# One weight sum of a seven-product matrix multiplication, computed on VectorE instead of GpSimd

## The chip, the cores and the metric

The kernel runs on one core of a Trainium2 chip. A core has five engines with a queue of instructions each: TensorE (PE) multiplies matrices into PSUM, VectorE (DVE), ScalarE (ACT) and GpSimd (POOL) work on tiles, and SyncE (SP) only issues transfers here. The metric is the device time of one execution in microseconds; lower is better.

## What is computed

One layer of a hybrid decoder, in float32, on 512 prompt rows and 32 sample rows. The change touches its last part, a gated MLP with a short causal convolution:

```python
h = _rmsnorm(x, g_pre_ffn) * (1 + sc_f) + sh_f
g, new_f = _causal_dwconv(h @ w_gate, st_f, conv_f_w)
f = silu(g) * (h @ w_up)
x = x + ga_f * _rmsnorm(f @ w_down, g_post_ffn)
```

The model width is 1024, the MLP's inner width 2816, that is 22 column blocks of 128. All 544 rows are processed together, in two halves of 272.

## The kernel before

Every float32 product is made of three matmuls: each operand is split into a high part (a copy rounded to the matmul's type, ScalarE, L242 for weights) and a low part (the difference, VectorE's or GpSimd's subtraction, L243), and `mm3` adds high x high, high x low and low x high (L246 to L248).

The first three column blocks of the gate and up matrices are multiplied plainly. From block 3 on each block j is a **pair**: the 2 x 2 arrangement of (gate or up) by (half of the rows) is computed by seven block products instead of eight, as in Strassen's scheme in Winograd's form. It needs four sums of weight blocks and four sums of activations. The weight sums S1 to S4 of a pair lie in one tile of 2048 columns, `gs`; the plain weights in another, `ga`. S1 and S3 are made by DMAs that add to what lies in `gs` (`s_dma`, issued by GpSimd, L1215 and L1216). S2 = S1 - W (a sign is folded into the stored weights) is an addition on VectorE (L1221), S4 is made from S2 by a further addition on GpSimd (L1222).

The weights of a pair are seven units of 512 columns (four 128x128 blocks), split by `w_prep(i, j)`: i = 0 takes units 0 and 1 from `ga`, i = 1 units 2 and 3 (the two DMA sums) from `gs`, i = 2 units 4 and 5 (S2 and S4) from `gs`, i = 3 unit 6 from `ga`. Each product is twelve matmuls of 128x272 on one unit (`p_step`), and the order on TensorE is products 1, 5, 7, 2, 6, 3, 4, on units 0, 3, 2, 1, 4, 5, 6. Product 1 of pair j + 1 follows product 4 of pair j.

The other engines work between these products in an order that is written out by hand; each engine takes its instructions in that order. For pair j of the loop it is, with the line that the profile shows:

- VectorE: the difference c21 of the pair before (L1280); the low half of units 4 and 5 (L243, called lo2 below); S2 of pair j + 1 (L1221); two taps of the convolution of the pair before (L1295) and two small ones (L1302); the low half of unit 6 (L243, zl); diff_75 (L1269); the gating product (L1314) and, for a pair of index below 6, the low half of a split of f (L1311); the low half of units 2 and 3 of pair j + 1 (lo1); c11 (L1272); the low half of units 0 and 1 of pair j + 1 (lo0); c12 (L1276, L1277).
- ScalarE: the high half before each low half (L242; for f L1310), copies of products out of PSUM (L1265), the first tap (L1290), a small tap (L1300), the silu of the pair before (L1305), a small state copy (L1286) that stands between c12 and the high half of units 4 and 5.
- GpSimd: S4 of pair j + 1 (L1222); a small copy (L1268); the two accumulating DMAs for pair j + 2 (L1215, L1216); c22 (L1283), which waits for ScalarE's copy of product 6; a small copy (L1287).

Pair 3 runs inside an order of its own, interleaved with the end of the plain blocks; there the steps `S` and `L0` make the sums of pairs 3 and 4. In the loop, pair j makes the sums of pair j + 1, from pair 4 to pair 20. So S2 and S4 are made 19 times, for pairs 3 to 21. Four tiles of the ring hold `ga` and `gs` of two pairs, and the plain loads of a further pair go into a tile when its last reader is done. After pair 21 the down projection follows on TensorE.

Of the kernel before, what the change touches and what calls it, by code (L numbers as in the profile page):

```python
# [104 lines left out]
def body(tc, nc, A):  # L105
# [3 lines left out]
    pe, act, dve, pool, sp = nc.tensor, nc.scalar, nc.vector, nc.gpsimd, nc.sync  # L109
# [1105 lines left out]
        pool.dma_start(t[:, :512], w[:, :512], accum_op=OP.add)  # L1215
        pool.dma_start(t[:, 512:1024], w[:, 1536:], accum_op=OP.add)  # L1216

    def s_add(j, eng=pool):

        w, t = ring.get(("ga", j)), ring.get(("gs", j))  # L1220
        dve.tensor_add(t[:, 1024:1536], t[:, 512:1024], w[:, :512])  # L1221
        eng.tensor_add(t[:, 1536:], t[:, 1024:1536], w[:, 512:1024])  # L1222
# [108 lines left out]
    def first_pair(k, i):  # L1331

        j = NA
        if k == "K":
            step(lambda: p_step(j, i))
        elif k == "X":
            a, r = {1: ("a", "p1"), 5: ("b", "p5"), 6: ("a", "u2")}[i]
            step(lambda: copy_out(j, a, r))
            if i == 6:
                step(lambda: acb.give(("a", j)))  # L1340
        elif k == "V":
            for fn in {7: (diff_75,), 1: (c11,), 2: (c22,), 3: (c12, states)}[i]:
                step(lambda fn=fn: fn(j))
        elif k == "R":
            n = j if i == 3 else j + 1
            step(lambda: w_prep(i, n), ("ga" if i in (0, 3) else "gs", n))
        elif i == 0:
            step(lambda: s_add(j + 1), ("ga", j + 1), ("gs", j + 1))
        else:
            step(lambda: s_dma(j + 2), ("gs", j + 2))  # L1350

    for w in FLOW.split():
        k, i = w[0], [int(c) for c in w[1:] if c.isdigit()]
        eng = pool if w[-1] == "p" else dve
# [14 lines left out]
        elif k == "u":  # L1369
            step(lambda i=i: up_ev(*i))  # L1370
        elif w == "To":
            step(t_open)
        elif k in "AB":
            step(lambda i=i, k=k, eng=eng: (t_add if k == "A" else t_split)(i[0], eng))
        elif k == "S":
            step(lambda: s_add(NA), ("ga", NA), ("gs", NA))
        elif k == "D":
            step(lambda i=i: s_dma(i[0]), ("gs", i[0]))
        elif k == "G":
            step(lambda i=i, eng=eng: w_prep(i[0], NA, eng), ("ga" if i[0] in (0, 3) else "gs", NA))  # L1380
        elif k == "s":
            step(lambda i=i: silu(*i))
        elif k == "d":
            s_adc(i[0])
        elif k == "f":
            step(ada_fin)
        elif k == "C":
            step(close_xy)
        elif k in "KXVRL":
            first_pair(k, i[0])  # L1390
        elif k == "N":
            step(lambda i=i: fill(int("".join(map(str, i)))))
        elif k == "P":
            step(lambda i=i[0]: (bk.append(Q["sc"][i]), acb.free.append(len(bk) - 1)))
        else:
            assert w == "o", w
            step(open_p3)
            step(lambda: ring.add_tiles([Q["x"][0].rearrange("p c t -> p (c t)")], ("adc",)))
# [20 lines left out]
    def s_sums(j):  # L1419
        step(lambda: s_add(j), ("ga", j), ("gs", j))  # L1420
# [53 lines left out]
    j = NFF - 1  # L1474
# [208 lines left out]
```

## Time and profile before

| | |
|---|---|
| median of three runs | 730.06 us (729.93 to 732.63) |
| the profiled execution's own time | 731.16 us |
| its span | 729.4 us |
| busy in the span: TensorE, VectorE, ScalarE, GpSimd | 95%, 66%, 48%, 36% |
| mean granted clock of TensorE | 0.985 of full speed |

The time of an execution holds the span, from the first to the last instruction of the profile, and something around it. "PE" is a matmul, "PEld" a weight load. Times of single instructions count from the span's start. A matmul's duration includes its way through the array, so that successive matmuls overlap; other instructions overlap their successor by up to 0.1 us in the same way.

### The profile page before, as it was taken

Reading aid. Unit: us, or ns where it says so; the run is one execution under the profiler, and the core shown is the slowest. Engines: PE = TensorE matmul, PEld = TensorE weight load, DVE = VectorE, ACT = ScalarE, POOL = GpSimd, SP = SyncE. Lnnn points to the kernel's source line nnn. Section 1 sums busy time; section 2 is a strip of 40 time slices with the busy share of each in tenths; the row PEclk is TensorE's granted clock in tenths of the full one; section 3 lists DMA queues with packets and bytes.
Section 4 is the critical chain, followed back from the end, with each engine's and each line's share of the span. In section 5 each row is a group of like instructions: output and inputs, shape, how many; then the busy total and the mean of one; then the engine's idle time right before and its main releaser. Section 6 shows DMA issues by size and latency. Waiting matters only on the chain.

```text
span 729.4 us, 15203 instructions
## 1 busy us (share of the span) xinstructions
PE 693.3 (95%) x6108; PEld 648.9 (89%) x6108; DVE 482.0 (66%) x902; ACT 351.2 (48%) x721; POOL 262.1 (36%) x294
## 2 busy tenths in 40 slices
PE   8997999899999989997997999999999999999994
PEld 8895778877879779987997999999999999999993
DVE  4859799787345463467878888888888882222353
ACT  4432454535453436572665566655665662322430
POOL 3753234222332353465434425444544100100224
PEclk9999999999999999999999999999999999999997
DMA  9979964668657546174436576677666626130012
GB/s 352 420 257 266 392 229 136 255 234 318 268 225 260 204 174 236 60 262 168 113 73 155 150 190 162 171 187 181 159 179 149 239 105 239 58 116 1 1 38 87
DMA packets 44231, 136.17 MB, mean 187 GB/s; under 512 B 12688, under 2 KB 15008, under 8 KB 37504
## 3 DMA queue, kind: packets, MB, share of 16 engines
q1 hardware_dynamic: 36160, 117.47, 45.3%
q0 software_dynamic: 7280, 17.03, 11.3%
q8 instruction: 48, 0.79, 0.4%
q10 hardware_dynamic: 720, 0.69, 0.3%
q14 instruction: 23, 0.19, 0.1%
HBM read 127.99 MB, written 7.18 MB: 185 GB/s over the span
## 4 chain that ended last, share of the span: by engine, by line
PE 75%; DVE 11%; POOL 4%; issue 3%; ACT 3%; DMA 2%; SPq 0%; POOLq 0%; ACTq 0%; DVEq 0%
PE bk L246 18%; PE bk L248 18%; PE bk L247 18%; PE bk L736 2%; PE sc L248 2%; PE sc L247 2%; PE sc L246 2%; DVE cv L755 2%; PE sc L696 2%; PE bk L668 1%; DVE stl L243 1%; DMA ring<-in_w_in 1%; PE bk L653 1%; ACT sth L242 1%; POOL rr L274 1%
## 5 line engine op out<-in xcount | busy, mean ns | idle before, releaser
L243 DVE TENSOR_TENSOR stl<-ring,sth 128x1024 fp32r<-128x1024 f32 (+2 forms) x96 | 111.7, 1170 | 84.4 <-ACT sth L242 82.9
L242 ACT ACTIVATE sth<-ring 128x1024 fp32r<-128x1024 f32 (+3 forms) x122 | 118.6, 997 | 58.4 <-PE bk L247 51.5
L247 PE MATMUL bk<-xl,sth 128*128 128x272 f32 x424 | 123.7, 292 | 0.0
L246 PE MATMUL bk<-xh,sth 128*128 128x272 f32 x360 | 108.6, 302 | 4.5 <-DVE bigq L565 3.8
L248 PE MATMUL bk<-zh,stl 128*128 128x272 f32 x360 | 104.6, 291 | 4.3 <-DVE stl L243 4.3
L246 PE MATMUL bk<-zh,sth 128*128 128x272 f32 x360 | 104.5, 290 | 1.2 <-ACT sth L242 1.2
L248 PE MATMUL bk<-xh,stl 128*128 128x272 f32 x360 | 105.6, 293 | 0.0
L247 PE MATMUL bk<-zl,sth 128*128 128x272 f32 x360 | 104.0, 289 | 0.1
L243 POOL TENSOR_TENSOR stl<-ring,sth 128x1024 fp32r<-128x1024 f32 (+1 forms) x26 | 60.8, 2339 | 91.0 <-ACT sth L242 83.2
L247 PEld LDWEIGHTS bk<-xl,sth 128*128 128x128 f32 x424 | 81.7, 193 | 0.1
L246 PE MATMUL bk<-th,sth 128*128 128x272 f32 x280 | 80.9, 289 | 0.0
L248 PE MATMUL bk<-th,stl 128*128 128x272 f32 x280 | 80.7, 288 | 0.0
L247 PE MATMUL bk<-xh,sth 128*128 128x272 f32 x280 | 80.3, 287 | 0.0
L246 PEld LDWEIGHTS bk<-xh,sth 128*128 128x128 f32 x360 | 69.5, 193 | 9.2 <-issue 4.1
L248 PEld LDWEIGHTS bk<-zh,stl 128*128 128x128 f32 x360 | 68.0, 189 | 5.2 <-DVE stl L243 5.2
L246 PEld LDWEIGHTS bk<-zh,sth 128*128 128x128 f32 x360 | 68.0, 189 | 2.1 <-ACT sth L242 1.7
L248 PEld LDWEIGHTS bk<-xh,stl 128*128 128x128 f32 x360 | 69.6, 193 | 0.0
L247 PEld LDWEIGHTS bk<-zl,sth 128*128 128x128 f32 x360 | 68.1, 189 | 0.3 <-POOL zl L1060 0.3
L247 PEld LDWEIGHTS bk<-xh,sth 128*128 128x128 f32 x280 | 52.8, 188 | 0.0
L248 PEld LDWEIGHTS bk<-th,stl 128*128 128x128 f32 x280 | 52.6, 188 | 0.0
L246 PEld LDWEIGHTS bk<-th,sth 128*128 128x128 f32 x280 | 52.6, 188 | 0.0
L755 DVE SCALAR_TENSOR_TENSOR cv<-apad,vec,cv 128x512 f32<-128x512 f32 x60 | 50.3, 838 | 1.7
(335 smaller groups left out, 1708.8 us busy)
## 6 DMA issues: line engine op xcount, KB each, us to landing
ring<-in_ada SPq DMA_DIRECT2D x15, 1024.0 KB, 9.5
ring<-in_w_gu SPq DMA_DIRECT2D x57, 256.0 KB, 5.4
ring<-in_kc SPq DMA_DIRECT2D x16, 896.0 KB, 4.9
ring<-in_vc SPq DMA_DIRECT2D x16, 896.0 KB, 6.8
ring<-in_w_dn SPq DMA_DIRECT2D x11, 1024.0 KB, 4.9
ring<-in_w_in SPq DMA_DIRECT2D x10, 1024.0 KB, 11.1
ring<-in_w_gu SPq DMA_DIRECT2D x19, 512.0 KB, 5.5
ring<-in_w_gu POOLq DMA_DIRECT2D x38, 256.0 KB, 5.8
```

The costliest lines, as they stand in the source:

```text
L242: act.activation(hi, r[:, a:a + n, :], AF.Copy)
L243: eng.tensor_sub(lo, r[:, a:a + n, :], hi.bitcast(F32))
L246: pe.matmul(acc, wh, rh, start=start, stop=False, skip_group_check=more)
L247: pe.matmul(acc, wh, rl, start=False, stop=False, skip_group_check=more)
L248: pe.matmul(acc, wl, rh, start=False, stop=stop, skip_group_check=more)
L274: pool.tensor_tensor(r[:, :3 * nh], v[:, :3 * nh], mhalf[:, :3 * nh], op=OP.pow)
L653: pe.transpose(tp[:, b * 128:b * 128 + 128], e[:, b * 128:b * 128 + 128], idn)
L668: pe.matmul(pv[64 * s:64 * s + 64, :128], P[f"vt{hp % 2}"][:, b, 64 * s:64 * s + 64], pts[s][:, b, :], start=b == 0, stop=b == qb, tile_po ...
L696: pe.matmul(sc2[32 * b:32 * b + 32, bank, off:off + n], P["bigq"][:, hp, 4 * g + b, :], rhs, start=first[bank] == i, stop=last[bank] == i, ...
L736: pe.matmul(pv[32 * b:32 * b + 32, :256], lhs, rhs, start=kb == 0, stop=kb == KB, tile_position=(0, 32 * b))
L755: dve.scalar_tensor_tensor(cv[:, j, :NP], ap_[:, j, k:k + NP], V("caw", j * WA + k), cv[:, j, :NP], op0=OP.mult, op1=OP.add)
```

## The change

S4 of each pair by seven products is computed by VectorE, directly behind S2, instead of by GpSimd. It is one default argument; no caller passes another engine:

```diff
-    def s_add(j, eng=pool):
+    def s_add(j, eng=dve):
 
         w, t = ring.get(("ga", j)), ring.get(("gs", j))
         dve.tensor_add(t[:, 1024:1536], t[:, 512:1024], w[:, :512])
         eng.tensor_add(t[:, 1536:], t[:, 1024:1536], w[:, 512:1024])
```

The second addition reads what the first writes. All other instructions keep their engines and their order.

## Rows read from the trace of the kernel before

**Rows 1.** The page: the span, and the busy time, share of the span and number of instructions of each engine.

```profile
span 729.4 us, 15203 instructions
PE 693.3 (95%) x6108; PEld 648.9 (89%) x6108; DVE 482.0 (66%) x902; ACT 351.2 (48%) x721; POOL 262.1 (36%) x294
```

**Rows 2.** Busy time by stretch: an early pair (411.40 to 422.90 us) and a late one. The stretch, its length, then the busy time of PE, PEld, DVE, ACT and POOL with their instructions, the granted clock, the DMA engines' share and GB/s.

```profile
411.40:422.90 11.50, 10.67 (x85) 10.45 (x84) 9.72 (x17) 6.73 (x12) 3.94 (x7) 1.00 0.61 149
...
465.00:475.50 10.50, 10.50 (x86) 10.50 (x86) 8.85 (x16) 6.19 (x11) 4.85 (x7) 1.00 0.74 173
```

**Rows 3.** The chain that ended last, in order of time, two pieces that stand at the same place of the pair, six pairs apart: start, us, what.

```profile
507.36 0.13 PE bk L247
...
570.56 0.13 PE bk L247
```

**Rows 4.** The timeline of TensorE, its matmuls that came after an idle time: start, us, instruction, and in brackets the idle time before it and what ended it. The first is in pair 5, the second in pair 7.

```profile
401.19 0.40 PE L248 MATMUL bk<-zh,stl 128*128 128x272 f32 x1 [1.69 <-DVE stl L243]
...
424.48 0.40 PE L248 MATMUL bk<-zh,stl 128*128 128x272 f32 x1 [0.86 <-DVE stl L243]
```

**Rows 5.** The timeline of VectorE, c12 at the end of pair 5, pair 6's end (424.35), pair 7 from lo2 (425.94) to its c12 (434.47), and lo0 in pair 8 (443.02). A row with x2 holds two instructions from the first's start to the second's end.

```profile
412.70 0.40 DVE L1276 TENSOR_TENSOR bk<-bk,u 128x240 f32<-128x240 f32 x1
...
424.35 0.40 DVE L1276 TENSOR_TENSOR bk<-sc,u 128x240 f32<-128x240 f32 x1
...
425.94 1.23 DVE L243 TENSOR_TENSOR stl<-ring,sth 128x1024 fp32r<-128x1024 f32 x1 [0.76 <-ACT sth L242]
427.09 0.69 DVE L1221 TENSOR_TENSOR ring<-ring,ring 128x512 f32<-128x512 f32 x1
427.69 1.53 DVE L1295 SCALAR_TENSOR_TENSOR gy<-bk,vec,gy 128x511 f32<-128x511 f32 x2
...
429.60 0.68 DVE L243 TENSOR_TENSOR zl<-ring,zh 128x512 fp32r<-128x512 f32 x1
...
431.42 1.22 DVE L243 TENSOR_TENSOR stl<-ring,sth 128x1024 fp32r<-128x1024 f32 x1
...
432.91 1.64 DVE L243 TENSOR_TENSOR stl<-ring,sth 128x1024 fp32r<-128x1024 f32 x1
434.47 0.40 DVE L1276 TENSOR_TENSOR bk<-bk,u 128x240 f32<-128x240 f32 x1
...
443.02 1.22 DVE L243 TENSOR_TENSOR stl<-ring,sth 128x1024 fp32r<-128x1024 f32 x1
```

**Rows 6.** The timeline of VectorE in a late pair, the two instructions before which it was idle longest.

```profile
456.12 0.44 DVE L1280 TENSOR_TENSOR fraw<-sc,u 128x272 f32<-128x272 f32 x1 [0.95 <-PE sc L248]
...
458.63 1.53 DVE L1295 SCALAR_TENSOR_TENSOR gy<-bk,vec,gy 128x511 f32<-128x511 f32 x2 [0.33 <-ACT gy L1290]
```

**Rows 7.** The timeline of GpSimd in pairs 7 and 8: S4, the first DMA issue, c22 of pair 7 and c22 of pair 8.

```profile
427.91 1.30 POOL L1222 TENSOR_TENSOR ring<-ring,ring 128x512 f32<-128x512 f32 x1 [2.81 <-issue]
...
429.29 0.85 POOL L1215 DMA_DIRECT2D ring<-in_w_gu  x1
...
432.70 0.77 POOL L1283 TENSOR_TENSOR fraw<-p,u 128x272 f32<-128x272 f32 x1 [1.67 <-DVE stl L243]
...
443.05 1.83 POOL L1283 TENSOR_TENSOR fraw<-p,u 128x272 f32<-128x272 f32 x1 [1.89 <-ACT u L1265]
```

**Rows 8.** The timeline of ScalarE: the high halves of units 2, 3 and of units 0, 1 of pair 8 (two instructions), the copy of product 6 of pair 7, and the high half of units 4 and 5 in pair 8.

```profile
430.35 1.99 ACT L242 ACTIVATE sth<-ring 128x1024 fp32r<-128x1024 f32 x2
432.24 0.37 ACT L1265 ACTIVATE u<-bk 128x272 f32<-128x272 f32 x1
...
434.98 1.06 ACT L242 ACTIVATE sth<-ring 128x1024 fp32r<-128x1024 f32 x1
```

**Rows 9.** The instructions that write or read the tile gy: the taps' durations in ns, least, median and longest, and first and last start.

```profile
L1295 DVE SCALAR_TENSOR_TENSOR gy<-bk,vec,gy x38: 740/749/750, 392.8 to 587.2; 128x511 f32<-128x511 f32 x19, 128x510 f32<-128x510 f32 x19
```

**Rows 10.** The timelines of VectorE and GpSimd around the sums of pair 3: two subtractions before, two after, and S4.

```profile
366.11 1.35 DVE L1210 TENSOR_TENSOR xh<-y,th 128x544 fp32r<-128x544 f32 x2
...
369.12 2.45 DVE L1210 TENSOR_TENSOR xh<-y,th 128x544 fp32r<-128x544 f32 x2
...
368.14 2.21 POOL L1222 TENSOR_TENSOR ring<-ring,ring 128x512 f32<-128x512 f32 x1 [2.25 <-DVE ring L1221]
```

**Rows 11.** The same timelines in pairs 3 and 4: GpSimd's memset in front of a DMA issue, S2 of pair 4, lo2 in pair 4, S2 of pair 5.

```profile
375.61 0.10 POOL L1139 MEMSET fraw<- 128x2 f32 x1 [3.98 <-DVE xl L1171]
...
382.19 0.69 DVE L1221 TENSOR_TENSOR ring<-ring,ring 128x512 f32<-128x512 f32 x1 [2.06 <-DMA ring<-in_w_gu]
...
390.82 1.23 DVE L243 TENSOR_TENSOR stl<-ring,sth 128x1024 fp32r<-128x1024 f32 x1 [0.78 <-ACT sth L242]
392.17 0.69 DVE L1221 TENSOR_TENSOR ring<-ring,ring 128x512 f32<-128x512 f32 x1
```

**Rows 12.** Who waited for whom between 363 and 600 us, of TensorE and of VectorE: us in total, times, longest.

```profile
PE bk L248 <- DVE stl L243: 4.3, 4, 1.7
...
DVE fraw L1280 <- PE bk L248: 6.6, 7, 1.0
```

**Rows 13.** The timeline of VectorE, lo0 for pair 21 and the first waits in pair 21.

```profile
569.18 1.22 DVE L243 TENSOR_TENSOR stl<-ring,sth 128x1024 fp32r<-128x1024 f32 x1
...
571.99 0.44 DVE L1280 TENSOR_TENSOR fraw<-bk,u 128x272 f32<-128x272 f32 x1 [0.95 <-PE bk L248]
...
574.50 0.75 DVE L1295 SCALAR_TENSOR_TENSOR gy<-bk,vec,gy 128x511 f32<-128x511 f32 x1 [0.94 <-ACT gy L1290]
```

## The prediction, made before the changed kernel ran

> **What bounds the kernel now.** I read the page first, then the busy time by stretch, then who waits for whom, then single instructions of a few pairs. The page [rows 1] shows TensorE busy for 95% of the span and VectorE for 66%; by this average VectorE has room. But the change touches one stage only, the pairs by seven products (about 363 to 585 us), and there the picture changes along the way. The stretches [rows 2] show one early and one late pair: in the early one TensorE is not full (10.67 of 11.50 us), in the late one it is (10.50 of 10.50), and VectorE works 9.72 and 8.85 us.
>
> The chain of work that ended last gives the late pace: the same place in the pair at 507.36 and, six pairs on, at 570.56 [rows 3], so 10.53 us for a pair, all on TensorE. The early pace is VectorE's: TensorE stands still for 1.69 and, two pairs on, for 0.86 us [rows 4] at the same place, the first matmul of a pair that needs the low half of weight unit 0. I call that low half lo0; it is one VectorE subtraction of 128x1024 (L243), like lo2 (S2 and S4's own split) at the pair's begin and lo1. The later of these stalls ends at 424.48, in pair 7. It is the last of the four times that TensorE waits for L243 in this stage [rows 12].
>
> VectorE's own loop explains both. Its first instruction on product 3 (L1276) comes at 412.70, 424.35 and 434.47 [rows 5]: 11.65 us for pair 6, which still carries a split of f for a small index, and 10.12 us for pair 7, which doesn't. 11.65 is above TensorE's 10.53, 10.12 below it; so TensorE waits up to pair 7 and VectorE afterwards: in a late pair it waits 0.95 us for TensorE and 0.33 us for ScalarE [rows 6]. The whole question is whether pair 7 and its successors stay under 10.53 us.
>
> **The change part by part.** *S4 leaves GpSimd.* There it takes 1.30 us and has waited 2.81 us for S2 [rows 7]. Its reader is ScalarE's split of S2 and S4 in the next pair, at 434.98 [rows 8], 5.8 us after S4's end, so its length was never on the path. Behind it in GpSimd's queue stand a small copy (L1268) and the two accumulating DMA issues for the pair after next; these can come up to 3 us earlier. That costs nobody: the issues at 429.29 ran beside VectorE's zl (429.60, two SBUF operands), which took the 0.68 us that S2 of the same size takes with no issue beside it [rows 5, 7].
>
> *S4 arrives on VectorE.* The nearest row is S2 itself: same shape, same tiles, 0.69 us, and the next instruction starts 0.60 us after its start [rows 5]. But S4 reads what S2 writes. The two taps L1295 are such a dependent couple: together 1.53 us at 0.75 us each [rows 5, 9], so the second starts 0.78 after the first, 0.03 after its end. S2 then holds S4 for 0.69 + 0.03 = 0.72 us, S4 lasts 0.60 to the next start: 0.72 us more per pair. Bounds: 0.60 if the dependence is free, 0.84 if the taps too had to wait for S4's end. I take 0.72, the price of the one dependent couple that the loop shows.
>
> The Trainium skill, VectorE: DVE Perf Modes, section The DRAIN you can't avoid, has a measurement in which a semaphore between chained VectorE operations costs nothing extra. By that, S4 would add 0.60 us and the sum below would be 4.4 us; by the row it is 0.72 and 6.6, and I keep the row, since its couple has a true dependence.
>
> *What hides it?* In the early pairs nothing. S4 stands right behind S2, and everything VectorE does up to lo0 stands behind S4 in order: the taps, the silu that ScalarE makes of them, lo1, lo0. The one idle time of that loop, 0.76 us before lo2 [rows 5], lies in front of S2 and is ScalarE's answer to L1276, so it moves along.
>
> **The sum, in order.**
> *Pair 3.* Here S4 on GpSimd (368.14, 2.21 us) overlapped a VectorE subtraction: the two L1210 from 369.12 took 2.45 us against 1.35 for the two before [rows 10]. That loss of 1.10 goes, 0.72 comes: -0.38. It carries on to GpSimd's memset at 375.61, which waits for VectorE, then to the DMA issue behind it, for which S2 of pair 4 waited 2.06 us [rows 11].
> *Pair 4's S4*, made in pair 3 behind that S2: +0.72, net +0.34 when pair 4 begins.
> *In pair 4* S2 of pair 5 starts 1.35 after lo2 [rows 11], elsewhere 1.15 [rows 5]; it waited 0.20 for the accumulating DMA, whose issue stood behind S4 on GpSimd and now comes earlier. -0.20 + 0.72 = +0.52, together +0.86.
> *Pairs 5 and 6* +0.72 each: TensorE's stall that ended at 424.48 ends 2.30 later.
> *Pair 7.* VectorE needs 10.12 + 0.72 = 10.84 us against 10.53. lo0 was ready at 432.91 + 1.64 = 434.55 [rows 5], now 434.55 + 2.30 + 0.72 = 437.57; TensorE wants it at 424.48 + 10.53 + 2.30 = 437.31. It waits again, 0.26: +2.6.
> *Pairs 8 to 20*, thirteen of them, each 10.84 - 10.53 = 0.31: +4.0, together +6.6. By the bounds: at 0.60 the same steps give 1.9 up to pair 7 and 13 x 0.19, 4.4; at 0.84, 3.3 and 13 x 0.43, 8.9.
> *Pair 21 and the down projection.* VectorE arrives there about 1.5 us later against TensorE than before: lo0 was ready at 570.40 [rows 13], wanted some 10.53 x 14 after 424.48, at 571.9. In that pair it has no S2 or S4 and waited 0.95 and 0.94 us [rows 13]; these cover it. +0; without that cover +1.5.
>
> Why pairs 8 to 20 don't return under 10.53: pair 7's 10.12 holds a lo0 of 1.64 us instead of 1.22 [rows 5]. It started 0.21 us after GpSimd's c22 (L1283, 432.70) [rows 7], and this distance is fixed while VectorE leads the loop, because both come from ScalarE's split at 430.35: c22 through the copy at 432.24 [rows 8], lo0 through lo1 at 431.42. In pair 8, where VectorE had caught up, c22 started 0.03 after lo0: lo0 took 1.22 and c22 1.83 [rows 5, 7]. So a pair costs VectorE 10.84 with the collision and 10.42 without, one above and one below 10.53. It stays on the side on which it is, and it comes from pairs 5 and 6 on the collided side. TensorE would have to hold c22's copy back; it ends that product 7.4 us after it got lo0 (1.4 for the rest of the first, four of 1.5), while the copy now comes 432.24 - 424.48 + 0.72 = 8.5 after.
>
> The profiled execution took 731.16 with a span of 729.4, 1.1 above the median of 730.06. The sum is a difference and I put it on the median: 730.06 + 6.6 = 736.7 us.
>
> **Rivals.**
> *A: the collision ends.* If c22 falls behind lo0 after pair 7, each pair has 10.42 us on VectorE and TensorE leads again: +2.6 only, 732.7. For it: it happened in pair 8 before. Against: the 0.21 was there in pairs 6 and 7 alike, and TensorE is 1.1 us too early. Chance 0.20.
> *B: GpSimd's S4 was costing VectorE.* Had every S4 held VectorE as the one of pair 3 did, the move would give 1.10 - 0.72 = 0.38 in each of the four pairs in which VectorE leads, and nothing later: 730.06 - 1.5 = 728.5, not slower. It decides from the point where S4 runs over a VectorE operation that reads two tiles in SBUF. The Trainium skill, SBUF — State Buffer, section SBUF: two separate sides, describes the port pair of VectorE and GpSimd as a lock that the first of such operations keeps; the trace agrees at lo0 (1.64 against 1.22) and at 369.12. Against B: in the loop S4 runs over the taps, which read PSUM, and all 38 of them took 740 to 750 ns [rows 9], those of the last pair without any S4 too. Chance 0.05.
> *C: more than the sum.* S4 holds the taps to its end (0.84 a pair): 730.06 + 8.9 = 739.0; or the tail's 1.5 isn't covered and pair 3's 0.38 isn't found: 738.6. For it: these are the terms seen least well. Against: S2's own end didn't hold the taps. Chance 0.07.
> My forecast keeps 0.68.
>
> **How the numbers follow.** Half a per cent, 3.65 us, is about what this measurement can tell from no change. Slower by more: the forecast, whose lower bound of 4.4 still counts, and C: 0.75. Within: A and half of B: 0.22. Faster: 0.03. The range reaches from A (732.7, less a little for its own spread) to just short of C: 732.3 to 738.8. The likeliest case alone, from a free dependence upward, has 734.4 to 738.8.
>
> **What the profile after would show.** L1222 on VectorE, nineteen times, some 0.68 us, starting 0.72 after S2. TensorE's waits for L243, four in all now [rows 12], in every pair to the last, 0.3 us each after pair 7. VectorE's waits for TensorE at L1280, 6.6 and as much again on the other bank [rows 12], gone. lo0 at 1.64 in nearly all pairs, c22 at 0.77 before it. The pair's pace 10.84 instead of 10.53. If lo0 stands at 1.22 from pair 8 on and the pace at 10.53, A is right; if S4 starts 0.60 after S2, the dependence was free; if the stall at pair 7 doesn't move by 2.3, an early term is wrong.

## The result, and the profile of the changed kernel

The changed kernel is slower by 0.8%: 737.94 us (736.37 to 740.05, four runs) against 729.99 (729.68 to 732.63, four runs) for the kernel before, a ratio of 1.0081 with a 95% interval of 1.0055 to 1.0106, so 4.0 to 7.7 us. The forecast was 736.7, 6.6 us more than before. Its profiled execution took 739.24 us.

The page of the changed kernel, the lines that answer to [rows 1]:

```profile
span 737.5 us, 15150 instructions
...
PE 698.6 (95%) x6108; PEld 651.6 (88%) x6108; DVE 496.8 (67%) x921; ACT 349.5 (47%) x721; POOL 226.4 (31%) x275
```

Nineteen instructions have gone from GpSimd to VectorE. VectorE's share of the span rises by one point only, and GpSimd's busy time falls by 35.7 us. The busy times alone would call this a change that costs nothing.

VectorE's timeline says otherwise; here pair 7 and a late pair, which answer to [rows 5]:

```profile
428.80 0.40 DVE L1276 TENSOR_TENSOR bk<-sc,u 128x240 f32<-128x240 f32 x1
...
430.39 1.23 DVE L243 TENSOR_TENSOR stl<-ring,sth 128x1024 fp32r<-128x1024 f32 x1 [0.75 <-ACT sth L242]
431.53 0.68 DVE L1221 TENSOR_TENSOR ring<-ring,ring 128x512 f32<-128x512 f32 x1
432.25 0.69 DVE L1222 TENSOR_TENSOR ring<-ring,ring 128x512 f32<-128x512 f32 x1
432.86 1.53 DVE L1295 SCALAR_TENSOR_TENSOR gy<-bk,vec,gy 128x511 f32<-128x511 f32 x2
...
438.06 1.64 DVE L243 TENSOR_TENSOR stl<-ring,sth 128x1024 fp32r<-128x1024 f32 x1
439.62 0.40 DVE L1276 TENSOR_TENSOR bk<-bk,u 128x240 f32<-128x240 f32 x1
...
513.81 1.64 DVE L243 TENSOR_TENSOR stl<-ring,sth 128x1024 fp32r<-128x1024 f32 x1
515.37 0.40 DVE L1276 TENSOR_TENSOR bk<-sc,u 128x240 f32<-128x240 f32 x1
...
524.63 1.64 DVE L243 TENSOR_TENSOR stl<-ring,sth 128x1024 fp32r<-128x1024 f32 x1
```

S4 (L1222) starts 0.72 us after S2, the taps 0.61 after S4. From c12 to c12 (L1276) pair 7 takes 439.62 - 428.80 = 10.82 us, and so does each of the eight pairs from 428.80 to 515.37, where the chain before had 10.53 [rows 3]. lo0, the last L243 ahead of c12, takes 1.64 us in the late pairs too.

GpSimd's timeline shows why; c22 in the two late pairs:

```profile
513.60 0.77 POOL L1283 TENSOR_TENSOR fraw<-p,u 128x272 f32<-128x272 f32 x1 [4.63 <-DVE stl L243]
...
524.41 0.77 POOL L1283 TENSOR_TENSOR fraw<-p,u 128x272 f32<-128x272 f32 x1 [4.95 <-DVE stl L243]
```

c22 starts 0.21 and 0.22 us ahead of lo0, as it did in pair 7 before [rows 7]. Before, this ended in pair 8; now it goes on to the end.

Who waited for whom between 363 and 608 us, TensorE's longest, and a late pair by busy time (columns as in [rows 2]):

```profile
PE bk L248 <- DVE stl L243: 5.4, 4, 1.5
```

```profile
515.37:526.19 10.82, 10.79 (x85) 10.57 (x84) 9.82 (x17) 6.06 (x11) 2.87 (x5) 1.00 0.66 169
```

VectorE's waits for TensorE at L1280 [rows 12] are gone from its list. But TensorE's waits for lo0 are still only four, and a late pair shows it busy for 10.79 of 10.82 us. TensorE's timeline shows where the 0.29 us are by which such a pair is longer:

```profile
525.87 0.29 PE L246 MATMUL bk<-zh,sth 128*128 128x272 f32 x1
526.00 0.28 PE L247 MATMUL bk<-zl,sth 128*128 128x272 f32 x1
526.32 0.40 PE L248 MATMUL bk<-zh,stl 128*128 128x272 f32 x1
526.56 0.29 PE L246 MATMUL bk<-zh,sth 128*128 128x272 f32 x1
```

The first matmul that needs lo0 (L248) starts 0.05 us after lo0's end (524.63 + 1.64) and 0.32 us after its predecessor, where others follow each other by 0.12 to 0.13, and itself takes 0.40 instead of 0.29, so that the next starts 0.24 after it. Together that is some 0.3 us. But a matmul's recorded 0.28 us reaches over most of the gap, and the list counts little of it as idle. The pace shows the loss, the list of waits doesn't.

**Where the time went.** TensorE runs the same matmuls in the same order in both kernels, so the start of the same matmul can be compared. I count it from the start of S2 of pair 3, because the two profiled executions differ before that: by 0.93 us at S2, which the change didn't cause. In each of the two TensorE was granted half its clock for a while where the other had all of it: in the execution of the kernel before at 130 to 133 us, in that of the changed kernel at 341 to 347 us, of which these rows show a part (the kernel before, then the changed one; the granted clock is the third column from the end). A second execution of the changed kernel, below, has the full clock there.

```profile
343.00:346.00 3.00, 3.00 (x25) 3.00 (x26) 2.42 (x4) 1.37 (x4) 2.82 (x7) 1.00 0.46 160
```

```profile
343.00:346.00 3.00, 3.00 (x15) 3.00 (x15) 2.96 (x5) 0.32 (x3) 2.84 (x5) 0.50 0.93 323
```

Counted so, TensorE is later than before by 1.66 us at product 1 of pair 4, by 2.14, 2.83 and 3.52 us in pairs 5, 6 and 7, by 3.72 in pair 8, by 7.27 ahead of the first matmul with lo0 of pair 21 (572 us), and by **7.57** from there to its last matmul. I call this last number the shift of the stage.

The changed kernel's execution has a time at half the clock inside the stage too, in pair 4; the kernel before has 1.00 there:

```profile
391.80:395.20 3.40, 3.40 (x17) 3.40 (x17) 2.64 (x6) 2.05 (x5) 1.86 (x4) 0.50 0.65 209
```

It makes TensorE 3.18 us late, but only until its next wait for lo0, in pair 5, where VectorE leads and 2.14 are left; so the shift doesn't contain it.

Executions of one kernel spread by some 5 us, and the longer ones have the lower mean granted clock: 30 of the kernel before go from 729.2 us at 0.985 to 734.5 us at 0.980. So the experiments below give the ratio of the times and, finer, the shift, which is of one profiled execution each. In every experiment the kernel before, run beside it, had the lower clock (medians of 0.980 to 0.982 against 0.9825 to 0.985). A line through its own runs gives 0.4 to 0.6 us for each 0.001 of clock, by which I estimate that the ratios put a run 0.2 to 2.4 us too low.

### The profile page after: what moved, and what is told of

Same layout as the page of the kernel before. It is cut to its first block, busy times and chain, and to the rows that moved or that the text cites. A ratio compares the mean times of both kernels' runs of the same rounds, so it can differ in the third digit from the quotient of the medians.

```text
span 737.5 us, 15150 instructions
## 1 busy us (share of the span) xinstructions
PE 698.6 (95%) x6108; PEld 651.6 (88%) x6108; DVE 496.8 (67%) x921; ACT 349.5 (47%) x721; POOL 226.4 (31%) x275
## 4 chain that ended last, share of the span: by engine, by line
PE 77%; DVE 11%; POOL 4%; issue 3%; ACT 3%; DMA 2%; SPq 0%; POOLq 0%; ACTq 0%; DVEq 0%
PE bk L248 18%; PE bk L246 18%; PE bk L247 18%; PE bk L736 2%; PE sc L248 2%; PE sc L246 2%; PE sc L247 2%; DVE cv L755 2%; PE sc L696 2%; PE bk L668 1%; DVE stl L243 1%; DMA ring<-in_w_in 1%; ACT sth L242 1%; PE bk L653 1%; POOL rr L274 1%
## 5 line engine op out<-in xcount | busy, mean ns | idle before, releaser
L243 DVE TENSOR_TENSOR stl<-ring,sth 128x1024 fp32r<-128x1024 f32 (+2 forms) x96 | 116.9, 1224 | 96.3 <-ACT sth L242 95.0
L248 PE MATMUL bk<-zh,stl 128*128 128x272 f32 x360 | 106.8, 297 | 5.8 <-DVE stl L243 5.4
L248 PE MATMUL bk<-xh,stl 128*128 128x272 f32 x360 | 104.9, 291 | 0.0
L243 POOL TENSOR_TENSOR stl<-ring,sth 128x1024 fp32r<-128x1024 f32 (+1 forms) x26 | 60.8, 2338 | 91.0 <-ACT sth L242 83.2
L248 PE MATMUL bk<-th,stl 128*128 128x272 f32 x280 | 80.7, 288 | 0.0
L248 PEld LDWEIGHTS bk<-zh,stl 128*128 128x128 f32 x360 | 68.7, 191 | 9.7 <-DVE stl L243 9.7
L248 PEld LDWEIGHTS bk<-xh,stl 128*128 128x128 f32 x360 | 68.9, 191 | 0.0
L248 PEld LDWEIGHTS bk<-th,stl 128*128 128x128 f32 x280 | 52.7, 188 | 0.0
## 6 DMA issues: line engine op xcount, KB each, us to landing
ring<-in_w_in SPq DMA_DIRECT2D x10, 1024.0 KB, 11.2
```

Of the source, the lines that this page charges most:

```text
L243: eng.tensor_sub(lo, r[:, a:a + n, :], hi.bitcast(F32))
L248: pe.matmul(acc, wl, rh, start=False, stop=stop, skip_group_check=more)
```

## The experiments

The theory: 0.72 us of S4 stand in VectorE's loop; they alone would be made up once VectorE is under TensorE's 10.53 us, but the collision of lo0 with c22 (1.64 instead of 1.22 us) keeps it at 10.82. The rival: a longer VectorE order costs by itself, or GpSimd's earlier DMA issues do. The ratios compare with runs of the kernel before on the same chip, the shifts with its first profiled execution.

**c22 moved.** The changed kernel, with c22 issued behind c12 and the small copies instead of ahead of them, so that it can't meet lo0:

```diff
-        do(c22, j)
         ...
         do(states, j)
+        do(c22, j)
```

> The changed kernel with c22 (GpSimd) put behind the small copies that follow c12, so that it starts after lo0 has ended. Theory (VectorE's loop is above TensorE's 10.53 us only because lo0 collides with c22): lo0 at 1.22 us in every pair, VectorE's loop 10.82 - 0.41 = 10.41 us, TensorE's pace 10.53 again from pair 7 on; 0.41 saved in pairs 4, 5 and 6 and 0.29 in each of the fourteen after: 1.2 + 4.0 = 5.2 under the changed kernel's 737.9, 732.7 us. Rival (the collision only accompanies it, the 0.72 us of added work sets the pace by itself): pace 10.8 us, 737 to 738 us.

Measured: 734.03 us, ratio 1.0021 (1.0004 to 1.0037); shift +2.26. VectorE's timeline, lo0 and the lo2 behind it:

```profile
415.00 1.22 DVE L243 TENSOR_TENSOR stl<-ring,sth 128x1024 fp32r<-128x1024 f32 x1
...
417.73 1.22 DVE L243 TENSOR_TENSOR stl<-ring,sth 128x1024 fp32r<-128x1024 f32 x1 [0.75 <-ACT sth L242]
```

lo0 (415.00) takes 1.22 like lo2 (417.73), in every pair. VectorE's pair is 11.93 us early, 10.41 from pair 7 on, until nine pairs later it has run up to TensorE, then 10.53. With S4 on VectorE and the collision gone, 5.3 of the 7.57 us are gone too, where 5.2 were expected; the rest arose in the early pairs.

**The same move without the change.**

> The kernel before, S4 on GpSimd, with the same move of c22. Theory: the three early pairs 4 to 6, in which VectorE leads, lose their collision, 0.41 each, and nothing else changes: 730.0 - 1.2 = 728.8 us. Rival (collisions cost VectorE nothing that the next wait doesn't give back): 730.0 us.

Measured: 729.65 us, ratio 0.9956 (0.9935 to 0.9978); shift -1.43. The early pairs take 11.23 instead of 11.65, pair 7 takes 9.70. TensorE's waits for lo0:

```profile
PE bk L248 <- DVE stl L243: 2.0, 4, 0.9
```

2.0 us instead of the 4.3 of [rows 12]. So the collision cost the kernel before as well, 0.42 us in each pair in which VectorE led.

**The sums first.** The changed kernel, with S2 and S4 ahead of lo2, so that they lie in VectorE's idle time before it ([rows 5], 0.76 us):

```diff
+        if new:
+            s_sums(j + 1)
         s_prep(2, j)
         do(copy_out, j, "a", "p1")
-        if new:
-            s_sums(j + 1)
```

> The changed kernel with S2 and S4 of the next pair put in front of lo2 on VectorE, into the 0.76 us in which VectorE waits for ScalarE after c12 and c21. Theory (what counts is the place in VectorE's loop, not its amount of work): lo2 starts some 2.1 us after c12 instead of 1.6, but 1.32 us of sums behind it are gone: the loop is 10.82 - 0.8 = 10.0 us with the collision still there, under 10.53, so TensorE sets the pace from pair 7 on; early pairs 11.5 instead of 12.33 us. 737.9 - 2.4 - 4.0 = 731.5 us. Rival (VectorE is simply too full with 0.69 us more per pair): no change, 737.9 us.

Measured: 731.63 us, ratio 0.9993 (0.9976 to 1.0010); shift +0.34. VectorE's timeline in a pair after pair 7:

```profile
442.15 1.82 DVE L243 TENSOR_TENSOR stl<-ring,sth 128x1024 fp32r<-128x1024 f32 x1
443.89 0.40 DVE L1276 TENSOR_TENSOR bk<-sc,u 128x240 f32<-128x240 f32 x1
...
444.65 0.44 DVE L1280 TENSOR_TENSOR fraw<-bk,u 128x272 f32<-128x272 f32 x1 [0.27 <-PE bk L248]
445.01 0.68 DVE L1221 TENSOR_TENSOR ring<-ring,ring 128x512 f32<-128x512 f32 x1
...
454.42 0.40 DVE L1276 TENSOR_TENSOR bk<-bk,u 128x240 f32<-128x240 f32 x1
```

Here lo0 still collides (1.82), and it does no harm: VectorE has 9.98 us of its own work in pair 7, and from pair 8 on it waits for TensorE (0.27 at L1280) and follows at 454.42 - 443.89 = 10.53. So against the kernel before, S4 on VectorE costs nothing that the times can tell, if the sums stand there. S2 has moved too, though, and no run has S2 alone in front with c22 in its old place, so this isn't S4's price in that order. With both sums in front of lo2, 0.82 and 0.84 us of each pair come back (12.33 to 11.51, 10.82 to 9.98): the 0.75 of idle time and a little more.

**S4 on VectorE only from pair 11's sums on, and only up to pair 8's.** The kernel before, with one line more in `s_add`:

```diff
+        eng = dve if j >= 11 else eng      # first run
+        eng = dve if j <= 8 else eng       # second run
```

> The kernel before with S4 on VectorE only for pairs 11 to 21 (made in pairs 10 to 20, where TensorE leads and VectorE waits for it); GpSimd makes the others. Theory (the late pairs stand by a hair: S4 uses up the 0.33 us wait and delays lo0 by 0.30, and lo0 led c22 by 0.28): the collision comes back, each of the eleven pairs costs VectorE 10.82 against 10.53, the first 1.5 us of that come out of lo0's lead, then TensorE stalls: 11 x 0.29 - 1.5 = 1.7 us over the kernel before; lo0 turns to 1.6 us from pair 10 on. Rival 1 (a fixed price of 0.29 per S4): 3.2 us over. Rival 2 (the 0.95 and 0.33 us of waits hold all of S4): no change, lo0 stays 1.22.

Measured: 732.05 us, ratio 1.0027 (1.0005 to 1.0049); shift +1.95. GpSimd and VectorE at the first S4 moved, and a pair later (c22 stands in line 1284 here):

```profile
462.25 0.76 POOL L1284 TENSOR_TENSOR fraw<-p,u 128x272 f32<-128x272 f32 x1 [2.92 <-ACT u L1266]
...
473.07 0.76 POOL L1284 TENSOR_TENSOR fraw<-p,u 128x272 f32<-128x272 f32 x1 [3.99 <-DVE stl L243]
```

```profile
462.27 1.82 DVE L243 TENSOR_TENSOR stl<-ring,sth 128x1024 fp32r<-128x1024 f32 x1
...
473.28 1.64 DVE L243 TENSOR_TENSOR stl<-ring,sth 128x1024 fp32r<-128x1024 f32 x1
```

In the kernel before, lo0 led c22 by 0.28 us in the same pair, pair 10; VectorE, then GpSimd:

```profile
463.84 1.21 DVE L243 TENSOR_TENSOR stl<-ring,sth 128x1024 fp32r<-128x1024 f32 x1
```

```profile
464.12 1.57 POOL L1283 TENSOR_TENSOR fraw<-p,u 128x272 f32<-128x272 f32 x1 [2.57 <-ACT u L1265]
```

The first S4 delays lo0 against it: c22 now starts 0.02 us ahead, and lo0 loses 0.6 us at once. From the next pair on the distance is 0.21 (0.32 once) and the pace 10.82. This execution was 0.40 us ahead of the kernel before when the first S4 came, so the eleven S4 add 2.35 us; the theory had 1.7 and the rival of a fixed price 3.2. Pair 10 with the first collision took 11.22 us, more than the 10.82 that the theory gave each. No early pair is needed to get onto the collided side; the first S4 tips the loop over, and with an S4 in every pair it stays there.

> The kernel before with S4 on VectorE only for pairs 3 to 8 (made up to pair 7), the others on GpSimd. Theory: all of the loss up to the first matmul with lo0 of pair 8 is there, 3.7 us by the changed kernel's trace counted from S2 of pair 3, and none after it, since the loop returns to 10.12 and then 9.7 us: 3.7 us over the kernel before at the end of the stage. Rival (each S4 costs the same share of the whole): 6 of 19 of 7.6, 2.4 us over.

Measured: 734.22 us, ratio 1.0044 (1.0026 to 1.0061); shift +3.01. VectorE's timeline after the last S4 moved (c21 stands in line 1281 here):

```profile
446.65 1.63 DVE L243 TENSOR_TENSOR stl<-ring,sth 128x1024 fp32r<-128x1024 f32 x1
...
456.75 1.22 DVE L243 TENSOR_TENSOR stl<-ring,sth 128x1024 fp32r<-128x1024 f32 x1
...
459.37 0.44 DVE L1281 TENSOR_TENSOR fraw<-sc,u 128x272 f32<-128x272 f32 x1 [0.95 <-PE sc L248]
```

The pairs take 12.33 and 10.83 while S4 is there, then 10.09, 9.70 and 10.53: lo0 returns to 1.22, VectorE waits for TensorE, and nothing is added after pair 8. Had the wait for S2 of pair 4 been 3.37 as in the changed kernel and not 2.54, the shift would have been 0.83 more, 3.84, near the expected 3.7.

**The DMA issues alone.** The step that the prediction had at nothing. In the changed kernel GpSimd no longer waits for S2 of pair 4, so it issues the DMAs for pair 5 right behind those for pair 4. In the kernel before the first of them came 8 us behind:

```profile
384.72 0.85 POOL L1215 DMA_DIRECT2D ring<-in_w_gu  x1
```

In the changed kernel, GpSimd and VectorE:

```profile
376.16 0.10 POOL L1139 MEMSET fraw<- 128x2 f32 x1 [4.61 <-DVE xl L1171]
...
377.31 1.18 POOL L1216 DMA_DIRECT2D ring<-in_w_gu  x1
378.73 1.21 POOL L1215 DMA_DIRECT2D ring<-in_w_gu  x1
```

```profile
367.04 1.34 DVE L1210 TENSOR_TENSOR xh<-y,th 128x544 fp32r<-128x544 f32 x2
368.32 0.68 DVE L1221 TENSOR_TENSOR ring<-ring,ring 128x512 f32<-128x512 f32 x1
...
370.77 1.35 DVE L1210 TENSOR_TENSOR xh<-y,th 128x544 fp32r<-128x544 f32 x2
...
384.06 0.69 DVE L1221 TENSOR_TENSOR ring<-ring,ring 128x512 f32<-128x512 f32 x1 [3.37 <-DMA ring<-in_w_gu]
```

S2 of pair 4 waits 3.37 us instead of 2.06 [rows 11]: the second accumulating DMA for pair 4, issued at 377.31, lands later. The run does this alone, on the kernel before: S2 and S4 become two steps, and `s_dma(j + 2)` is issued between them.

```diff
-            step(lambda: s_add(j + 1), ("ga", j + 1), ("gs", j + 1))
+            step(lambda: s_add(j + 1, parts="2"), ("ga", j + 1), ("gs", j + 1))
             ...
+            step(lambda: s_add(j + 1, parts="4"), ("ga", j + 1), ("gs", j + 1))
```

> The kernel before with one thing of the changed kernel: in pair 3 the two accumulating DMAs for pair 5 are issued before S4 of pair 4 and not behind it (S4 stays on GpSimd, S2 on VectorE). Theory (they run beside those for pair 4, on which S2 of pair 4 waits, and make them land 1.3 us later): S2 of pair 4 waits 3.4 us instead of 2.06, 730.0 + 1.3 - 0.2 = 731.1 us. Rival (the later landing in the changed kernel was an accident of that execution): wait about 2.06, 730.0 us.

Measured: 731.88 us, ratio 0.9988 (0.9976 to 1.0000); shift +0.80. By the ratio the run isn't slower at all; its median clock was 0.9835 against 0.9805 for the kernel before, so the loss is shown by the profiled execution only. GpSimd's and VectorE's timelines (S2 stands in line 1222 here):

```profile
375.28 1.18 POOL L1216 DMA_DIRECT2D ring<-in_w_gu  x1
376.69 1.21 POOL L1215 DMA_DIRECT2D ring<-in_w_gu  x1
```

```profile
381.71 0.69 DVE L1222 TENSOR_TENSOR ring<-ring,ring 128x512 f32<-128x512 f32 x1 [3.06 <-DMA ring<-in_w_gu]
```

The wait is 3.06 us with S4 still on GpSimd, so the longer wait doesn't need S4 on VectorE. The later pairs keep their old pace.

**The changed kernel once more,** for the size of that wait.

> The changed kernel once more, beside the same runs of the kernel before. Theory: S2 of pair 4 again waits some 3.3 us for its DMA, since the issue for pair 5 follows 2 us behind it, and the stage counted from S2 of pair 3 is 7.3 to 7.6 us longer than in the kernel before. Rival (the later landing in the first profile was chance): the wait is near 2.06 and the stage 6.3 us longer.

Measured: 738.78 us, ratio 1.0100 (1.0074 to 1.0126); shift +6.35. S2 of pair 4 on VectorE:

```profile
380.46 0.69 DVE L1221 TENSOR_TENSOR ring<-ring,ring 128x512 f32<-128x512 f32 x1 [2.14 <-DMA ring<-in_w_gu]
```

The wait is 2.14 us this time: the expectation fell, and its rival, that the later landing of the first profile was chance, held for this execution. TensorE is late by 0.43, 0.92, 1.61 and 2.30 us in pairs 4 to 7, and by 6.35 at the stage's end. The wait varies from one execution to the next, and with it the whole difference between the two shifts, 7.57 and 6.35.

**All three remedies on the kernel before.** c22 moved as above, S2 first for j > 4, and S4 of pair 3 on VectorE.

```diff
+        eng = dve if j == NA else eng
...
+        if new and j > 4:
+            s_sums(j + 1)
         s_prep(2, j)
         do(copy_out, j, "a", "p1")
-        if new:
+        if new and j == 4:
             s_sums(j + 1)
```

> S4 on GpSimd as before except that of pair 3, which goes to VectorE; c22 behind the small copies after c12; and from pair 5 on S2 in front of lo2, in VectorE's 0.76 us of waiting for ScalarE. Theory: c22's move 1.4 us less as measured, pair 3's collision of 1.10 for 0.72, 0.4 less, S2 out of the loop of the two early pairs 5 and 6, 0.6 each: 3.0 us under the kernel before; early pairs 11.2 (pair 4) and 10.6 us. Rival (S2 in front waits for its accumulating DMA and holds lo2 up): pairs 5 and 6 no shorter than 11.2 and the total 1.8 under or less.

Measured: 733.69 us, ratio 1.0033 (1.0015 to 1.0050); shift -2.07 at pair 7, but +4.38 at the end. VectorE's waits:

```profile
DVE ring L1221 <- DMA ring<-in_w_gu: 29.8, 14, 2.8
```

From pair 8 on S2 stands so early that it waits some 2 us for its accumulating DMA in every pair. The expectation of -3.0 fell. The rival's wait came, but from pair 8 on; pairs 5 and 6 took 10.96 us, where the theory had 10.6 and the rival 11.2. What held them up is the collision once more, of S2 with the moved c22, which starts 0.04 us ahead of it:

```profile
399.91 1.29 DVE L1221 TENSOR_TENSOR ring<-ring,ring 128x512 f32<-128x512 f32 x1
```

So S2 first is good only where the DMAs are ahead:

```diff
-        if new and j > 4:
+        if j in (5, 6, 7):
             s_sums(j + 1)
         ...
-        if new and j == 4:
+        if new and j not in (5, 6, 7):
             s_sums(j + 1)
```

> S4 on GpSimd except that of pair 3; c22 behind the small copies after c12; S2 in front of lo2 only in pairs 5 to 7, where its DMA has landed in time, and behind lo2 from pair 8 on. Theory: TensorE's last stall ends 2.07 us earlier, counted from S2 of pair 3, as it did with S2 in front everywhere, and keeps it, since the 2 us of waiting for the DMA that came from pair 8 on are gone: 2.07 us under the kernel before. Rival (the wait for the DMA comes from c22's move, not from S2's place): waits of some 2 us stay and the stage is longer than before.

Measured: 729.24 us, ratio 0.9958 (0.9939 to 0.9977); shift -2.34. The waits of S2 shrink to

```profile
DVE ring L1221 <- DMA ring<-in_w_gu: 4.2, 4, 2.1
```

so the rival fell, and the version is faster than both kernels: than the one before by 0.4% by the ratio, by 2.34 us (0.3%) by the shift. By the time that is no more than c22's move alone gave (0.9956). The two shifts, -2.34 against -1.43, are of one execution each; what tells the versions apart is the step of TensorE's lead from pair 5 to 6 and from 6 to 7, 0.69 and 0.70 us here, 0.41 and 0.42 with c22's move alone.

**Both remedies on the changed kernel:** c22 moved, and the sums first.

> The changed kernel (S4 on VectorE everywhere) with both moves: c22 behind the small copies after c12, S2 and S4 in front of lo2. Theory: early pairs 11.51 - 0.41 = 11.1 us, TensorE's pace from pair 7 on, so 0.34 - 3 x 0.41 = 0.9 us under the kernel before, counted from S2 of pair 3, with the same wait of S2 of pair 4 as then: S4's place costs, not its work. Rival (0.69 us more work on VectorE has to be paid somewhere): 2 us or more over it.

Measured: 732.36 us, ratio 0.9995 (0.9973 to 1.0018); shift +0.67, where -0.9 was expected. c22 of pair 5 on GpSimd, and VectorE from c12 of pair 5 to S2 in pair 6:

```profile
415.20 0.78 POOL L1283 TENSOR_TENSOR fraw<-p,u 128x272 f32<-128x272 f32 x1
```

```profile
414.48 0.41 DVE L1276 TENSOR_TENSOR bk<-bk,u 128x240 f32<-128x240 f32 x1
...
415.25 1.28 DVE L1221 TENSOR_TENSOR ring<-ring,ring 128x512 f32<-128x512 f32 x1
```

The two moves meet: c22 no longer runs ahead of lo0, but 0.05 us ahead of S2, which takes 1.28 us instead of 0.68. The collision has only changed its victim: pair 4 takes 11.08 us, as expected, but pairs 5 and 6 take 11.68. Beside the same runs of the kernel before, the version with S4 on GpSimd had 0.9958 and -2.34. So with the order mended for either, S4 on VectorE was still the slower place, by 3.0 us of shift; 1.0 of them is S2 of pair 4, which waited 3.09 us here and 2.10 there.

## Why the prediction was right, and where it was not

*S4's price.* Predicted 0.72 us a pair; measured 0.72 from S2 to S4 and then 0.61 to the taps against 0.60 from S2 to the taps before [rows 5], so 0.73 at that place, in all loop pairs alike. A whole pair grew a little less, from 10.12 to 10.82, since some hundredths came back elsewhere in the loop. The price of the dependent couple was the right row. That the dependence were free, 0.60, is excluded, and so is 0.84, by which the taps would wait for S4's end.

*Pair 3.* Predicted -0.38. The two L1210 after S2 take 1.35 us instead of 2.45 [rows 10]. The memset comes 0.55 us later than before (376.16 against 375.61 [rows 11]), S2 of pair 3 0.94 later (368.32 against 367.38, the row below): -0.39.

```profile
367.38 0.68 DVE L1221 TENSOR_TENSOR ring<-ring,ring 128x512 f32<-128x512 f32 x1
```

*"That costs nobody"*, said of GpSimd's earlier DMA issues, is the step that failed. The prediction looked for their cost on VectorE and not at the landing of the transfers issued just ahead. S2 of pair 4 waited longer for that landing, by 3.37 - 2.06 = 1.3 us in the profiled execution and by 0.1 in the second. Over all twelve profiles the landing took 5.2 to 5.7 us without the early issue and 5.5 to 6.7 with it.

*Pairs 4 to 7.* Predicted +0.34, +0.86, +1.58 and +2.30. The second execution, in which that wait was short, has 0.43, 0.92, 1.61 and 2.30; the first has the same steps (0.48, 0.69, 0.69) on top of a larger start. That 2.30 is met exactly is luck: a start larger by 0.09 and three steps smaller by 0.03 each.

*Pair 7 and thirteen more.* Predicted 10.84 us a pair and +4.3 in all; measured 10.82, so 0.29 each, and +4.05 in both executions (3.52 to 7.57, 2.30 to 6.35). The collision that stays is shown as the cause by two runs: without it the pace returns to 10.53, and with S4 from pair 11 on alone it sets in at once. Rival A, that it ends of itself, didn't happen. The argument for its staying, that the distance between c22 and lo0 is fixed while VectorE leads, holds to 0.01 us in the rows shown (0.21 and 0.22).

*The sum.* Predicted +6.6; 7.57 in the first execution and 6.35 in the second, and 5.9 by the first ratio (0.0081 of 730), with 4.0 to 7.7 as its interval, 7.3 by the second. That it lies so near is in part luck: the fourteen late pairs were taken 0.25 us too large, and the landing at nothing. The tail added nothing, as predicted: the last step to 7.57 comes with lo0 of pair 21.

*Rival B*, a gain, fell: outside pair 3 the rows show no cost of GpSimd's S4 to VectorE, whose early pairs grew from 11.65 to 12.33 us, nearly by the whole price of S4.

*What the profile was to show.* TensorE's waits for L243 "in every pair to the last" aren't in the list. The stalls are there, as the pace shows, but too short to be listed as waits. VectorE's waits at L1280 (6.6 us before, and 5.7 on the other bank) are gone, as forecast.

## What to carry to other kernels

An instruction goes to the engine whose loop has room at that place of the order, not to the one with the lower average: VectorE was at 66%, and 0.72 us in its loop cost some 6 us, while with both sums one step earlier in the order the kernel took as long as before. Where two instructions collide on a fixed distance, the loop has two paces, here 10.82 and 10.41 us around a bound of 10.53, and a small delay can decide which of them it keeps; compute both before moving anything, and look for what a moved instruction collides with next. When an instruction leaves a queue, ask of every DMA issue behind it which transfer it now runs beside.

## What the runs showed of the hardware that was not expected

The order of arrival decides a collision. A VectorE subtraction or addition of two SBUF tiles that starts 0.02 to 0.22 us behind a GpSimd one of 0.77 us ends late: lo0 takes 1.64 at a distance of 0.21 and 1.82 at 0.02, S2 1.28 instead of 0.68 at 0.05. So they lose 0.42, 0.60 and 0.60 us, each 0.13 to 0.15 less than GpSimd's instruction has left at that point (0.56, 0.75 and 0.73). The Trainium skill, SBUF — State Buffer, section SBUF: two separate sides, calls the shared port pair an exclusive lock that goes to whichever starts first for the whole instruction. The rows agree in who wins and in how the loss falls with the distance; the loss itself is that much shorter than the whole rest of the instruction.

An accumulating DMA of GpSimd tends to land later when two more are issued close behind it. From issue to landing the second one for pair 4 took 5.2 to 5.7 us in the five profiles in which the next stood some 8 us behind, and 5.5 to 6.7 us in the seven in which they stood 1.4 us behind. The groups touch at 5.5 to 5.7. In those five the second one for pair 5, with none so close behind it, took 6.2 to 6.9, so the distance isn't all, and what sets the size stays open; no run separates the issue from the traffic of the transfers.
